# Row sums of mixing weights: added up by transfers in DRAM instead of products with ones

## Chip, cores and metric

The kernel runs on one core of a Trainium2 chip. The metric is the device time of one execution, in microseconds; the runs shown are three, and their median is the time before.

## What is computed

One layer of a streaming encoder: RMSNorm, one wide input projection, a sliding-window attention branch, a gMLP branch with spatial gating, gates, an output projection and a last RMSNorm. All in float32, with 1024 tokens and 1024 channels. The part that matters here is the spatial gating:

```python
def chunked_spatial_gating(u, v, w_s, b_s, ln_g, ln_b):
    v = layernorm(v, ln_g, ln_b)                      # (x - mu) * r * ln_g + ln_b
    vb = v.reshape(B, nb, SG_BLOCK, SG_GROUPS, SG_GROUP_WIDTH)
    mask = jnp.asarray(cidx[None, :] <= cidx[:, None])   # chunks of 64
    w = jnp.where(mask[None], w_s, jnp.zeros_like(w_s))
    mixed = jnp.einsum('gij,bnjgc->bnigc', w, vb) + jnp.transpose(b_s)[None, None, :, :, None]
    return u * mixed.reshape(B, S, SG_WIDTH)
```

Since `ln_b` is the same for every position j, its share of `mixed` is `ln_b[c]` times the sum of `w[g, i, j]` over j. So the kernel mixes only the normalized values and keeps, for each group g and row i, a bias: (row sum) x `ln_b` + `sg_b`. The row sums are 8 x 128 numbers, wanted in all 128 partitions (channels). The weights come as `sg_w[j, g, i]`; for j of 64 and above, only i of 64 and above counts.

## The kernel before

Every large product is a float32 product made of three products of split values (a rounded high part and a rest), and products of 2x2 blocks are done by a scheme of seven products on sums and differences (`b11`, `t1`, `t2`, `b21`, `t3`, `b22`, `t4`). A value is split by a cast on ACT (L176, `wh` or `T_..h`) and a subtraction on DVE (L177, `wl` or `T_..l`).

The stage that the change touches lies between 55 and 125 us. Until 94 us the projection of `vs`, the gMLP's gated input, is computed: L793 with weights `s1`, `s4`, then `late_product` (L1005) three times, for `t2`, `t3` and `t4`. Each call has two halves of the weights (c) and four token tiles (t), six matmuls each, and accumulates into four PSUM banks (`accs`: two of `ps_mm`, two of `ps_tp`). Between the calls' tiles other work is dealt out from a list (`aside`): splits of the next weights and forms, GELU on ACT, statistics on DVE. After the second half of each tile a step (`to_x12`, L1017, and `to_x22`, L1020) takes the bank's content away on DVE, and only then may the next call add to that bank. So in DVE's queue stand, one behind the other: the four `T_t2l`, the `wl` of the second half of t2, the `wl` of s3's first half, four `T_t3l`, then statistics and `to_x12` in turn.

From 94 us on `gemm_pair` (L371) does the projection of `u`, four pairs of seven products. Between its products `hook` (L1073) takes two entries at a time from a list `late`: second-half statistics of eight tiles, `normalize` (L1082), `bias_of` (L1089), and `mix` (L1105), which multiplies 128x128 blocks of normalized values by the mixing weights, adds the bias and stores the product with `u` to DRAM.

The row sums before: the mixing weights (tile `wT`, loaded at L969) get their masked corner set to zero (L1046), are split like any other weight (L1048), and four matmuls (L1059) multiply a 128x128 tile of ones (L1003) by the high and the low parts, 512 columns at a time. That leaves the row sums in all 128 partitions of two PSUM banks (`ps_sc`), which `bias_of` reads.

Transfers: SP issues plain loads and stores, in its own order. POOL issues the transfers that add (`accum_op`). Before 55 us these make sums of weights (L618: `T_t4h`, `T_t3h`, `T_t3l`) and sums of forms of the input (L618: `x` <- `T_t4l` at `add_on` in `second_tile`, `xh` <- `xh` in `raw_t2`). From 63 us on POOL adds up weights in DRAM for later phases (`early`, L316, one step at every second tile of `late_product`). An engine's queue runs in order: a POOL transfer that waits for another to land holds up all that POOL issues behind it. Eight semaphores are used in turn for the transfers of each kind of queue, so a transfer also waits for the one that had its semaphore before.

The order in which the instructions of an engine stand is not the order of the code: a scheduler places them by its own estimate of when their inputs are ready, and `after` (L99) adds constraints by hand.

Of the kernel before, what the change touches and what calls it, by code (L numbers as in the profile page):

```python
# [24 lines left out]
F32 = mybir.dt.float32  # L25
F32R = mybir.dt.float32r
AF = mybir.ActivationFunctionType
ALU = mybir.AluOpType
PSUM = bass.MemoryType.PSUM

P = 128
D = 1024
S = 1024
KC = D // P
HALF = 512
# [17 lines left out]
def hybrid_tile(  # L53
# [16 lines left out]
    nc = tc.nc  # L70
# [8 lines left out]
    def nm(s):  # L79
        count[0] += 1  # L80
        return f"{s}_{count[0]}"

    def bank(tag, dt=F32):
        return psum.tile([P, 512], dt, name=nm("ps_" + tag), tag="ps_" + tag, bufs=2)

    def mtile(shape, dt, tag, bufs, pool=None):
        return (pool or main).tile(shape, dt, name=nm(tag), tag=tag, bufs=bufs)

    def scratch(name, shape=(D, S)):
        return dram.tile(list(shape), F32, name=name)  # L90
# [4 lines left out]
    def xtile():  # L95
        return mtile([P, HALF], F32, "x", 5)


    def after(second, first):  # L99

        tc.add_manual_dep(
            second.ins,
            first.ins.name,
            mybir.DependencyInfo(mybir.DependencyClass.NoSync, mybir.DependencyReason.DATA),
            reason="order",
        )
# [6 lines left out]
    ident = const.tile([P, P], F32, name="ident")  # L113
# [21 lines left out]
    k_dr = scratch("k_dr", (P, 4, S))  # L135
    v_dr = scratch("v_dr", (NT, P, 2, 3 * HD))
    s1_dr = scratch("s1_dr")
    z_dr = scratch("z_dr")
    gs_dr = scratch("gs_dr")
    ga_dr = scratch("ga_dr")  # L140
# [28 lines left out]
    def split(hi, lo, src, minus=False):  # L169
        if minus:  # L170
            hi_of.append(nc.scalar.mul(hi, src, -1.0))
            return nc.vector.scalar_tensor_tensor(
                lo, src, -1.0, hi.bitcast(F32), op0=ALU.mult, op1=ALU.subtract
            )
        else:
            hi_of.append(nc.scalar.copy(hi, src))  # L176
            lo_of.append(nc.vector.tensor_sub(lo, src, hi.bitcast(F32)))  # L177
            return lo_of[-1]
# [32 lines left out]
    def copy_to(dst, src):  # L211
        nc.sync.dma_start(dst, src)
# [39 lines left out]
    def half_of(half):  # L252
        return slice(half * HALF, (half + 1) * HALF)
# [100 lines left out]
    def product(acc, part, form, fresh, last=True):  # L354
        wh, wl = part
        bh, bl = form
        for k in range(4):
            ks = slice(k * P, (k + 1) * P)
            for n, (lt, rt) in enumerate(
                ((wh[:, ks], bh[:, k, :]), (wh[:, ks], bl[:, k, :]), (wl[:, ks], bh[:, k, :]))  # L360
            ):
                nc.tensor.matmul(  # L362
                    acc,
                    lt,
                    rt,
                    start=fresh and k == 0 and n == 0,
                    stop=k == 3 and n == 2,
                    skip_group_check=True,
                )

    def gemm_pair(b, finish, hook=lambda: None, second="o"):  # L371

        n = done[0]
        done[0] += 1
        acc = bank("mm")[:]
        x11, x12, x22 = xtile(), xtile(), xtile()
        product(acc, ready[n, 0], b["b11"], True)
        pace[0] = nc.scalar.copy(x11[:], acc)  # L380
        hook()
        t5 = bank("o")[:]
        product(t5, ready[n, 2], b["t1"], True)
        pace[0] = nc.scalar.mul(x22[:], t5, -1.0)
        hook()
        product(acc, ready[n, 3], b["t2"], False)
        pace[0] = nc.scalar.copy(x12[:], acc)
        split_next()
        hook()
        t2 = bank(second)[:]  # L390
        product(t2, ready[n, 1], b["b21"], True)
        term[0] = term_of_x11[0] = nc.vector.tensor_add(x11[:], x11[:], t2)
        finish(0, 0, x11, x11[:], 1.0)
        split_next()
        hook()
        product(acc, ready[n, 4], b["t3"], False)
        term[0] = nc.vector.tensor_sub(x22[:], x22[:], acc)
        finish(1, 1, x22, x22[:], 1.0)
        hook()
        product(t5, ready[n, 5], b["b22"], False)  # L400
        term[0] = nc.vector.tensor_add(x12[:], x12[:], t5)
        finish(0, 1, x12, x12[:], 1.0)
        split_next()
        hook()
        product(acc, ready[n, 6], b["t4"], False)
        finish(1, 0, xtile(), acc, -1.0)
        split_next()
        hook()
# [102 lines left out]
    def part_of_early(every=2):  # L511
        hooks[0] += 1
        if early and hooks[0] % every == 0:
            early.pop(0)()
# [28 lines left out]
    pool = outer.enter_context(tc.tile_pool(name="mixing", bufs=1))  # L543
# [71 lines left out]
    casts, lows, turns, scalings, squares = [], [], [], [], []  # L615

    def add_on(dst, src):
        return nc.gpsimd.dma_start(dst, src, accum_op=ALU.add)  # L618
# [127 lines left out]
    def pair_of_w():  # L746
        return mtile([P, D], F32R, "wh", 3), mtile([P, D], F32R, "wl", 3)
# [5 lines left out]
    def split_w(name, c, src=None, behind=False):  # L753
        hi, lo = pair_of_w()
        (split_behind if behind else split)(hi[:], lo[:], flat(two_k(raws[name], c)) if src is None else src)
        keep_w(name, c, hi, lo)
# [211 lines left out]
    mix_w = mtile([P, KC, P], F32, "wT", 1, pool)  # L968
# [23 lines left out]
    def statistics(t, half):  # L992
        return nc.vector.bn_stats(stats[:, t, half, :], xh[:, t, half_of(half)])
# [5 lines left out]
            for i in range(2):  # L999
                after(statistics(t + i, 0), lows[-1])  # L1000

    ones = mtile([P, P], F32R, "ones", 1, pool)
    after(nc.vector.tensor_scalar(ones[:], ident[:], 0.0, 1.0, op0=ALU.mult, op1=ALU.add), lows[-1])  # L1003

    def late_product(name, weight, done, aside):  # L1005
        for c in range(2):
            for t in range(4):
                pace[0] = vs_product(accs[t], name, t, weight, False, cs=(c,))
                if t % 2:
                    part_of_early(1)  # L1010
                if c:
                    done(t)
                if aside:
                    aside.pop(0)()
# [16 lines left out]
    def part_of(name, t):  # L1031
        form_of(name, t, by_k(nf12[t][:] if name == "t3" else raw_b21(t)))
        if name == "t3" and t == 3:
            after(kept[3], casts[-1])

    late_product(
        "t2",
        "s2",
# [2 lines left out]
        + [lambda t=t: part_of("t3", t) for t in range(4)]  # L1041
        + [lambda: gelu_of(0), lambda: gelu_of(2)],
    )
    row_sums = [bank("sc") for half in range(2)]
    split_w("s3", 1)
    after(nc.vector.memset(mix_w[64:128, :, 0:64], 0.0), lows[-1])  # L1046
    wh, wl = pair_of_w()
    split(wh[:], wl[:], mix_w[:].rearrange("p g i -> p (g i)"))  # L1048
    late_product(
        "t3",  # L1050
        "s3",
# [2 lines left out]
        + [lambda t=t: part_of("t4", t) for t in range(4)]  # L1054
        + [lambda: split_w("a22", 0, a22[0][:]), lambda: gelu_of(4), lambda: gelu_of(6)],
    )
    for half in range(2):
        for n, part in enumerate((wh, wl)):
            nc.tensor.matmul(row_sums[half][:], ones[:], part[:, half_of(half)], start=n == 0, stop=n == 1)  # L1059
    split_w("a22", 1, a22[1][:])  # L1060
    part_of_early(1)
    begin_job()
# [8 lines left out]
    late = []  # L1071

    def hook():  # L1073
        for _ in range(2):
            if late:
                late.pop(0)()

    def statistics_of(t):
        statistics(t, 1)
        nc.vector.bn_aggr(mv[:, t, :], stats[:, t])  # L1080
# [8 lines left out]
    def bias_of(half):  # L1089

        wT = mix_w[:, half * 4 : half * 4 + 4, :]
        bg = first_bias
        if half:
            bg = mtile([P, 4, P], F32, "bias", 1, pool)
            nc.sync.dma_start(bg[:].rearrange("p g i -> p (g i)"), sg_b[half_of(half)].partition_broadcast(P))
        for gg in range(4):
            g = half * 4 + gg
            nc.vector.scalar_tensor_tensor(
                bg[:, gg, :], row_sums[half][:, gg * P : (gg + 1) * P], lb_sb[:, g : g + 1], bg[:, gg, :], op0=ALU.mult, op1=ALU.add
            )  # L1100
        return bg, wT
# [26 lines left out]
    def both():  # L1128
        part_of_early(1)
        hook()  # L1130

    late.extend(lambda t=t: statistics_of(t) for t in range(NT))
    late.append(normalize)
    for m in range(0, KC, 2):

        def finish(i, half, q, src, sign, m=m):
            nc.scalar.activation(q[:], src, AF.Gelu, scale=sign)
            late.append(lambda: mix(m + i, half, q))

        if m % 4 == 0:  # L1140
            late.append(lambda m=m: bias.append(bias_of(m // 4)))
        gemm_pair(hb, finish, both)
    while late:
        late.pop(0)()
# [5 lines left out]
    pool = stage.enter_context(tc.tile_pool(name="keys", bufs=1))  # L1150
# [44 lines left out]
    pool = stage.enter_context(tc.tile_pool(name="queries", bufs=1))  # L1195
# [210 lines left out]
    pool = stage.enter_context(tc.tile_pool(name="attention", bufs=1))  # L1406
# [234 lines left out]
    pool = stage.enter_context(tc.tile_pool(name="later", bufs=1))  # L1641
# [384 lines left out]
    for p in range(4):  # L2026
        n, t, acc, x11 = N_PAIRS + p, T_ORDER[p], accs[p], firsts[p]
# [93 lines left out]
        for e in range(2):  # L2121
            cs = slice(e * wide, (e + 1) * wide)
            part = bank("sc")[:, 0:wide]
# [95 lines left out]
```

## Time and profile before

| | |
|---|---|
| runs | 894.76, 895.32, 896.27 us (median 895.32) |
| profiled execution | 894.85 us, its span 893.0 us |
| granted TensorE clock | 0.999 |
| transfers | 212.40 MB, mean 238 GB/s |

How to read the lines that follow. Times are microseconds from the start of the span. PE is the engine of matmuls, DVE and ACT work on vectors, POOL and SP mostly issue transfers ("POOLq", "SPq" are their sequencers). A row of a timeline has start, duration, engine, line, operation, what is written <- read, the count, and in brackets how long the engine had been idle before and what ended that. Matmuls are pipelined: the row of one is longer than the distance to the next. A landing is the time from the issue of a transfer to its completion.

### The profile page before, as it was taken

Reading aid. Unit: us, or ns where it says so; the run is one execution under the profiler, and the core shown is the slowest. Engines: PE = TensorE matmul, PEld = TensorE weight load, DVE = VectorE, ACT = ScalarE, POOL = GpSimd, SP = SyncE. Lnnn points to the kernel's source line nnn. Section 1 sums busy time; section 2 is a strip of 40 time slices with the busy share of each in tenths; the row PEclk is TensorE's granted clock in tenths of the full one; section 3 lists DMA queues with packets and bytes.
Section 4 is the critical chain, followed back from the end, with each engine's and each line's share of the span. In section 5 each row is a group of like instructions: output and inputs, shape, how many; then the busy total and the mean of one; then the engine's idle time right before and its main releaser. Section 6 shows DMA issues by size and latency. Waiting matters only on the chain.

```text
span 893.0 us, 13163 instructions
## 1 busy us (share of the span) xinstructions
PE 883.5 (99%) x4117; PEld 731.3 (82%) x4117; DVE 684.9 (77%) x1362; ACT 581.0 (65%) x1189; POOL 151.4 (17%) x217
## 2 busy tenths in 40 slices
PE   9999999999999999999999999999999999999996
PEld 6888888888888888888888888888888888888885
DVE  7879966566686778888878888847796578579886
ACT  6875523334445489999889999955685385467443
POOL 3332222203030001111211011101121121110012
PEclk9999999999999999999999999999999999999999
DMA  9997888958778767888776789989899789998533
GB/s 329 221 276 211 269 204 172 175 153 266 246 253 289 213 186 190 209 190 195 176 229 215 239 223 236 237 286 378 317 292 375 271 232 257 298 309 282 178 119 118
DMA packets 131410, 212.40 MB, mean 238 GB/s; under 512 B 12778, under 2 KB 59882, under 8 KB 131340
## 3 DMA queue, kind: packets, MB, share of 16 engines
q1 hardware_dynamic: 108808, 148.62, 50.2%
q0 software_dynamic: 22384, 62.67, 31.6%
q8 instruction: 33, 0.54, 0.2%
q14 instruction: 37, 0.30, 0.1%
q10 hardware_dynamic: 148, 0.27, 0.1%
HBM read 146.37 MB, written 86.11 MB: 260 GB/s over the span
## 4 chain that ended last, share of the span: by engine, by line
PE 93%; ACT 3%; DVE 2%; issue 1%; DMA 1%; POOL 0%; SPq 0%; ACTq 0%
PE ps_mm L362 41%; PE ps_o L362 26%; PE ps_tp L362 7%; PE ps_sc L362 3%; PE ps_tp L793 2%; PE ps_o L793 2%; PE ps_mm L793 2%; PE ps_sc L1438 2%; PE ps_tp L1511 2%; PE ps_tp L1109 2%; PE ps_o L1546 2%; PE ps_sc L793 1%; PE ps_o L1551 1%; PE ps_sc L663 1%; ACT pr L1466 1%
## 5 line engine op out<-in xcount | busy, mean ns | idle before, releaser
L176 ACT CAST wh<-s 128x1024 fp32r<-128x1024 f32 (+1 forms) x79 | 79.4, 1006 | 77.4 <-PE ps_mm L362 27.7
L177 DVE TENSOR_TENSOR wl<-wr,wh 128x512 fp32r<-128x512 f32 (+1 forms) x77 | 72.0, 937 | 56.1 <-ACT wh L176 55.2
L177 DVE TENSOR_TENSOR wl<-s,wh 128x1024 fp32r<-128x1024 f32 (+1 forms) x79 | 92.5, 1170 | 9.6 <-ACT wh L176 9.6
L176 ACT CAST wh<-wr 128x512 fp32r<-128x512 f32 (+1 forms) x77 | 63.0, 819 | 55.3 <-PE ps_mm L362 30.7
L362 PE MATMUL ps_o<-T_t1h,wh 128*128 128x512 f32 x148 | 57.9, 391 | 0.0
L362 PE MATMUL ps_o<-T_t1h,wl 128*128 128x512 f32 x148 | 57.7, 390 | 0.0
L362 PE MATMUL ps_o<-T_t1l,wh 128*128 128x512 f32 x148 | 57.6, 389 | 0.0
L1444 ACT COPY sl<-ps_sc 128x384 f32<-128x384 f32 (+2 forms) x128 | 51.9, 456 | 7.0 <-DVE sm L1450 7.0
L1466 ACT ACTIVATE pr<-pr,sm 128x192 f32<-128x192 f32 (+2 forms) x128 | 56.2, 444 | 0.1
L1450 DVE CUSTOM_DVE_ANT_0 pr<-sl,nsink_sb 128x192 f32<-128x192 f32 (+2 forms) x128 | 48.0, 399 | 10.0 <-ACT sl L1444 8.9
L362 PE MATMUL ps_mm<-T_b11h,wh 128*128 128x512 f32 x140 | 55.0, 393 | 0.0
L362 PE MATMUL ps_mm<-T_t3h,wh 128*128 128x512 f32 x140 | 54.9, 392 | 0.0
L362 PE MATMUL ps_mm<-T_b11l,wh 128*128 128x512 f32 x140 | 54.6, 390 | 0.0
L362 PE MATMUL ps_mm<-T_t3h,wl 128*128 128x512 f32 x140 | 54.6, 390 | 0.0
L362 PE MATMUL ps_mm<-T_b11h,wl 128*128 128x512 f32 x140 | 54.6, 390 | 0.0
L362 PE MATMUL ps_mm<-T_t2l,wh 128*128 128x512 f32 x140 | 54.6, 390 | 0.0
L362 PE MATMUL ps_mm<-T_t2h,wh 128*128 128x512 f32 x140 | 54.6, 390 | 0.0
L362 PE MATMUL ps_mm<-T_t3l,wh 128*128 128x512 f32 x140 | 54.6, 390 | 0.0
L362 PE MATMUL ps_mm<-T_t2h,wl 128*128 128x512 f32 x140 | 54.5, 389 | 0.0
L362 PE MATMUL ps_mm<-T_t4h,wh 128*128 128x512 f32 x136 | 53.5, 393 | 0.0
L362 PE MATMUL ps_mm<-T_t4h,wl 128*128 128x512 f32 x136 | 53.1, 390 | 0.0
L362 PE MATMUL ps_mm<-T_t4l,wh 128*128 128x512 f32 x136 | 53.0, 389 | 0.0
(425 smaller groups left out, 2454.2 us busy)
## 6 DMA issues: line engine op xcount, KB each, us to landing
wr<-in_w_dram SPq DMA_DIRECT2D x86, 256.0 KB
sums<-in_w_dram POOLq DMA_DIRECT2D x20, 512.0 KB, 7.4
s<-sums SPq DMA_DIRECT2D x20, 512.0 KB
q_hl<-qhl SPq DMA_DIRECT2D x16, 512.0 KB
q<-q_hl SPq DMA_DIRECT2D x64, 128.0 KB
y_dr<-x POOLq DMA_DIRECT2D x28, 256.0 KB, 6.8
g<-in_w_dram POOLq DMA_DIRECT2D x12, 512.0 KB, 6.5
wr<-in_w_dram SPq DMA_DIRECT2D x11, 512.0 KB
```

Of the source, the lines that this page charges most:

```text
L176: hi_of.append(nc.scalar.copy(hi, src))
L177: lo_of.append(nc.vector.tensor_sub(lo, src, hi.bitcast(F32)))
L362: nc.tensor.matmul(acc, lt, rt, start=fresh and k == 0 and n == 0, stop=k == 3 and n == 2, skip_group_check=True,)
L663: turns.append(nc.tensor.transpose(pt[:, i * P : (i + 1) * P], xt[:, k * P : (k + 1) * P], ident[:]))
L793: mm = nc.tensor.matmul(acc[:], lt, rt, start=fresh and k == 0 and n == 0, stop=stops and k == 3 and n == terms[-1], skip_group_check=True,)
L1109: nc.tensor.matmul(pm[:, t * P : (t + 1) * P], xh[:, half * 4 + t, g * P : (g + 1) * P], bias[-1][1][:, g % 4, :], start=True, stop=True,)
L1438: nc.tensor.matmul(sc, q_of[:, c, i * P : (i + 1) * P], kt[:, :, lo:hi], start=True, stop=True)
L1444: copies.append(nc.scalar.copy(two, sc))
L1450: nc.vector.tensor_tensor_reduce(v, two[:, 0, :], two[:, 1, :], 1.0, nsk[:, i : i + 1], op0=ALU.add, op1=ALU.min, accum_out=nmax[:, c, i : ...
L1466: e = nc.scalar.activation(v, v, AF.Exp, bias=nmax[:, c, i : i + 1], scale=-1.0, accum_out=sums[:, c, i : i + 1])
L1511: nc.tensor.transpose(dst, pr[:, i, block * P : block * P + width], ident[:])
L1546: nc.tensor.matmul(po[:, first], va[1][:, vs], a[:, n, first], start=n == 0, stop=n == 1, skip_group_check=True)
```

## The change

The row sums are no longer products. In DRAM, a scratch `rs_dr` of 64 x 1024 gets the rows j = 0 to 63 by a plain copy (SP); the rows 64 to 127 are added to it by a transfer of POOL, only for i of 64 and above (which is the mask). Then six adding transfers of POOL halve the number of rows, 64 to 32, 16, 8, 4, 2 and 1; each needs the one before. At last two loads (SP) bring the 512 sums of each half from DRAM into a tile `rs` of 128 equal rows. The tile `ones`, the split of the mixing weights and the four matmuls are dropped. `bias_of` reads `rs` in place of PSUM. The tile `rs` has one buffer, so the second load waits until the first half's bias is made.

```diff
-    ones = mtile([P, P], F32R, "ones", 1, pool)
-    after(nc.vector.tensor_scalar(ones[:], ident[:], 0.0, 1.0, op0=ALU.mult, op1=ALU.add), lows[-1])
+    def add_rows(n):
+        return lambda: nc.gpsimd.dma_start(rs_dr[0:n], rs_dr[n : 2 * n], accum_op=ALU.add)
+
+    def first_rows():
+        copy_to(rs_dr[:], sg_w[0:64].rearrange("j g i -> j (g i)"))
+
+    def second_rows():
+        add_on(rs_dr[:].rearrange("j (g i) -> j g i", g=KC)[:, :, 64:P], sg_w[64:P, :, 64:P])
+
+    def load_row_sums(half):
+        row_sums.append(mtile([P, HALF], F32, "rs", 1, pool))
+        nc.sync.dma_start(row_sums[half][:], rs_dr[0][half_of(half)].partition_broadcast(P))
+
+    row_sums = []
+    first_rows()
+    adding = [None, second_rows]
+    for n in (32, 16, 8, 4, 2):
+        adding += [None, add_rows(n)]
...
                 if t % 2:
                     part_of_early(1)
+                elif adding:
+                    step = adding.pop(0)
+                    if step is not None:
+                        step()
...
-    row_sums = [bank("sc") for half in range(2)]
     split_w("s3", 1)
     after(nc.vector.memset(mix_w[64:128, :, 0:64], 0.0), lows[-1])
-    wh, wl = pair_of_w()
-    split(wh[:], wl[:], mix_w[:].rearrange("p g i -> p (g i)"))
...
-    for half in range(2):
-        for n, part in enumerate((wh, wl)):
-            nc.tensor.matmul(row_sums[half][:], ones[:], part[:, half_of(half)], start=n == 0, stop=n == 1)
...
+    assert not adding
+    late.append(add_rows(1))
     late.extend(lambda t=t: statistics_of(t) for t in range(NT))
+    late.insert(8, lambda: load_row_sums(0))
     late.append(normalize)
...
+        if m == 2:
+            late.append(lambda: load_row_sums(1))
```

What the scheduler makes of it, at two places. First POOL's queue before 63 us. `x` and `xh` are the sums of forms of the input, `T_t4h` the sum that becomes `s3`. Before:

```order
L618 DMA x_145<-T_t4l_400 128x512
L618 DMA xh_120<-xh_120 128x512
L618 DMA x_146<-T_t4l_400 128x512
L618 DMA xh_120<-xh_120 128x512
L618 DMA T_t4h_529<-in_w_dram 128x1024 x2
L618 DMA x_147<-T_t4l_400 128x512
L618 DMA xh_120<-xh_120 128x512
L618 DMA x_148<-T_t4l_400 128x512
L618 DMA xh_120<-xh_120 128x512
```

And in the changed kernel (there the numbers of tiles are higher by one; `rs_dr` is the scratch of the row sums, and the form tells how many rows are added):

```order
L619 DMA rs_dr<-in_sg_w_dram 512x64
L1004 DMA rs_dr<-rs_dr 16x2048
L1004 DMA rs_dr<-rs_dr 16x1024
L1004 DMA rs_dr<-rs_dr 16x512
L619 DMA x_146<-T_t4l_401 128x512
L619 DMA xh_121<-xh_121 128x512
L1004 DMA rs_dr<-rs_dr 16x256
L619 DMA x_147<-T_t4l_401 128x512
L1004 DMA rs_dr<-rs_dr 16x128
L619 DMA xh_121<-xh_121 128x512
L619 DMA T_t4h_530<-in_w_dram 128x1024 x2
L1004 DMA rs_dr<-rs_dr 16x64
```

So the seven adds stand much earlier than in the code: the first four ahead of all sums of forms, the last ahead of the third `x`.

Second, the load of the sums on SP and its reader on DVE. SP before, from the loads of the first weights of `u` on (`wr`):

```order
L212 DMA wr_909<-in_w_dram 128x512 x2
L212 DMA wr_910<-in_w_dram 128x512 x2
L212 DMA wr_991<-in_w_dram 128x512 x2
L212 DMA wr_992<-in_w_dram 128x512 x2
L212 DMA wr_1181<-in_w_dram 128x512 x2
```

SP in the changed kernel:

```order
L213 DMA wr_903<-in_w_dram 128x512 x2
L213 DMA wr_904<-in_w_dram 128x512 x2
L1014 DMA rs_1096<-rs_dr 128x512
L1014 DMA rs_1238<-rs_dr 128x512
L213 DMA wr_987<-in_w_dram 128x512 x2
L213 DMA wr_988<-in_w_dram 128x512 x2
```

DVE before, from the first `wl` of s2 on:

```order
L682 TENSOR_TENSOR wl_690<-T_t3h_163,wh_689 128x1024
L673 SCALAR_TENSOR_TENSOR T_t2l_694<-xh_120,T_t2h_693 128x4x128 x4
L1003 TENSOR_SCALAR ones_735<-ident 128x128
L177 TENSOR_TENSOR wl_728<-T_t3h_163,wh_727 128x1024
L177 TENSOR_TENSOR wl_744<-T_t4h_529,wh_743 128x1024
```

DVE in the changed kernel:

```order
L683 TENSOR_TENSOR wl_691<-T_t3h_164,wh_690 128x1024
L674 SCALAR_TENSOR_TENSOR T_t2l_695<-xh_121,T_t2h_694 128x4x128 x4
L1113 SCALAR_TENSOR_TENSOR bias_628<-rs_1096,lb_sb,bias_628 128x128 x4
L178 TENSOR_TENSOR wl_729<-T_t3h_164,wh_728 128x1024
L178 TENSOR_TENSOR wl_744<-T_t4h_530,wh_743 128x1024
```

The four bias operations of the first half now stand ahead of the second `wl` of s2; before, they stood among the statistics of the second halves (93 to 95 us). On PE the four products with ones are gone, and the first four mixings stand one product later: two behind the first pair's `t4` instead of ahead of it, two behind the second pair's `b11`.

More of the change, by code (lines that the diff above doesn't have):

```diff
@@ L137, in hybrid_tile @@
     s1_dr = scratch("s1_dr")
+    rs_dr = scratch("rs_dr", (64, D))
     z_dr = scratch("z_dr")
```

## Prediction

> **What bounds the kernel now.** I read the page first: the busy times, then the shares of the chain of waits.
>
> ```profile
> PE 883.5 (99%) x4117; PEld 731.3 (82%) x4117; DVE 684.9 (77%) x1362; ACT 581.0 (65%) x1189; POOL 151.4 (17%) x217
> PE 93%; ACT 3%; DVE 2%; issue 1%; DMA 1%; POOL 0%; SPq 0%; ACTq 0%
> ```
>
> PE works in 883.5 of 893.0 us and carries 93% of the chain. So whatever PE no longer does comes off the time, and whatever makes PE wait is added to it. Next come the stages around the change (the view by windows; its columns are PE, weight loads, DVE, ACT and POOL, each with its count, then clock, DMA share and GB/s).
>
> ```profile
> 60.00:66.00 6.00, 6.00 (x28) 4.97 (x27) 3.94 (x5) 6.00 (x10) 0.76 (x1) 1.00 1.07 333
> 66.00:72.00 6.00, 6.00 (x28) 4.96 (x27) 6.00 (x10) 2.77 (x3) 1.94 (x3) 1.00 0.85 255
> 72.00:83.00 11.00, 11.00 (x50) 9.10 (x49) 10.77 (x17) 7.13 (x9) 2.87 (x5) 1.00 0.67 186
> ```
>
> PE has no gap there at full clock, but from 66 us on DVE has none either (6.00 of 6.00, 10.77 of 11.00). A DVE that is held up before 66 us has nothing to catch up with except its lead over PE.
>
> **What is removed.** The timeline of PE gives the four products with ones, and two points that I need later.
>
> ```profile
> 66.02 0.62 PE L793 MATMUL ps_mm<-wl,T_t2h 128*128 128x512 f32 x2
> 75.08 0.61 PE L793 MATMUL ps_tp<-wh,T_t3h 128*128 128x512 f32 x2
> 81.89 0.39 PE L1059 MATMUL ps_sc<-wh,ones 128*128 128x512 f32 x1
> 82.82 0.62 PE L793 MATMUL ps_mm<-wh,T_t4h 128*128 128x512 f32 x2
> ```
>
> The rows say 0.39 us each, but they overlap: from the first of the four (81.89) to the product behind them (82.82) it is **0.93 us**, and that is all that PE saves. The split of the weights also goes: one cast on ACT, and one subtraction on DVE that the next fence shows at 75.35 (1.22 us). Neither engine is waited for at that place, so both count nothing by themselves; DVE's gives it back some lead after 75 us.
>
> **What is moved: the bias.** The order shows the four bias operations of the first half where `ones` was made, ahead of the `wl` that the second half of the t2 product reads. In the timeline of DVE:
>
> ```profile
> 58.45 0.22 DVE L1003 TENSOR_SCALAR ones<-ident 128x128 fp32r<-128x128 f32 x1
> 61.85 1.23 DVE L177 TENSOR_TENSOR wl<-T_t3h,wh 128x1024 fp32r<-128x1024 f32 x1 [3.19 <-ACT wh L176]
> 72.18 0.68 DVE L1017 TENSOR_TENSOR xh<-xh,ps_tp 128x512 f32<-128x512 f32 x1
> 75.35 1.22 DVE L177 TENSOR_TENSOR wl<-wT,wh 128x1024 fp32r<-128x1024 f32 x1
> 94.38 0.29 DVE L1098 SCALAR_TENSOR_TENSOR bias<-ps_sc,lb_sb,bias 128x128 f32<-128x128 f32 x1
> 94.59 0.68 DVE L993 BATCH_NORM_STATS2 bn<-xh 128x6 f32<-128x512 f32 x1
> ```
>
> A bias operation takes 0.29 us, with the next start 0.21 us behind it, so four take about 0.9 us, and they can't start before the load of the row sums has landed, at T. DVE's queue is in order, so T + 0.9 is when the `wl` starts that started at 61.85.
>
> What does that cost PE? Two leads are to be compared. This `wl` ends at 63.08 and PE first reads it at 66.02: a lead of 2.94 us. Behind it DVE runs without a gap up to the add that ends at 72.86, which empties the bank that PE's row at 75.08 writes: a lead of 2.22 us. (The other adds of that phase have more.) The smaller decides: PE's stall is T + 0.9 - 61.85 - 2.22, that is **T - 63.2 us**, nothing if T is earlier. Later DVE gets its 1.22 us back, so I look for no further loss.
>
> **When does T come?** The load stands behind a chain. On POOL: the add of the lower rows, and six adds, each waiting until the one before has landed. In POOL's timeline these follow the row at 34.77, so they start at about 35.6 us; in the order the transfers of the other rows stand between or behind them.
>
> ```profile
> 34.77 0.85 POOL L618 DMA_DIRECT2D T_t3l<-T_t3h  x1 [1.72 <-DVE T_b22l L677]
> 35.34 1.15 POOL L618 DMA_DIRECT2D x<-T_t4l  x1
> 45.31 0.86 POOL L618 DMA_DIRECT2D T_t4h<-in_w_dram  x1 [3.01 <-DMA T_t4h<-in_w_dram]
> 54.01 0.86 POOL L618 DMA_DIRECT2D xh<-xh  x1 [1.43 <-DVE xh L720]
> ```
>
> How long a link takes is read from the landings, asked for one issue at a time (the add at 35.34, the one at 45.31, the one at 54.01), and, for a small transfer on a quieter queue, from the copies of the keys (32 KB, 16 of them):
>
> ```profile
> x<-T_t4l POOLq DMA_DIRECT2D x1, 256.0 KB, 5.7
> T_t4h<-in_w_dram POOLq DMA_DIRECT2D x1, 512.0 KB, 9.7
> xh<-xh POOLq DMA_DIRECT2D x1, 256.0 KB, 10.2
> DMA to landing us min/median/max: 2.2/2.9/3.7
> ```
>
> None of these is a small add from DRAM to DRAM, so its price lies between 2.2 and 10.2 us. The first link goes behind the T_t3l adds as the 256 KB add did, and I give it that add's 5.7 us: 41.3. The next two find the queue nearly empty but the DMA engines busy; 4 us each, nearer to 2.9 than to 5.7: 49.3. Then the two x and xh adds, which before were issued from 35.34 on, go out, and the last three links stand in one queue with four such adds (1.05 MB) and the two T_t4h adds (1.05 MB). What that queue moves is in the DMA view, here 42 to 50, 52 to 60, 60 to 68 and 68 to 70 us (packets, MB, share; q0 is POOL's queue, q1 the hardware queue that SP issues to):
>
> ```profile
> q1 hardware_dynamic: 462, 1.71, 60.7%
> q0 software_dynamic: 312, 0.55, 41.2%
> q0 software_dynamic: 618, 1.56, 101.8%
> q1 hardware_dynamic: 620, 0.12, 14.1%
> q1 hardware_dynamic: 1104, 1.78, 61.2%
> q1 hardware_dynamic: 2, 0.00, 0.3%
> ```
>
> With the hardware queue on small packets POOL's queue moves 1.56 MB in 8 us, so 2.1 MB take 10.8 us and the last add lands near 49.3 + 10.8 + 2.2 = 62.3. With large packets beside it (1.71 MB in 462) POOL's queue makes only 0.55 MB in 8 us, and some 5 us more are added: 62 to 67 us.
>
> Then the load itself. SP has it behind the loads of the first weights of the next phase (SP's timeline, and a row of its waits):
>
> ```profile
> 48.50 0.35 SPq L969 DMA_DIRECT2D wT<-in_sg_w_dram  x1
> 59.84 0.33 SPq L212 DMA_DIRECT2D wr<-in_w_dram  x1
> 80.12 9.33 SPq L212 DMA_DIRECT2D wr<-in_w_dram  x4
> SPq L212 <- DMA sink_sb<-in_sinks_dram: 2.1, 1, 2.1
> ```
>
> Before, SP issued the fourth of these loads at 59.84, was done with that at 60.2, and waited 2.1 us for the sinks, whose semaphore the load now reuses: it can't be issued before 62.3. And the hardware queue goes in order: from 52 to 60 us it moved 0.12 MB of small rows, with the 512 KB of mixing weights (issued at 48.5) and the rest waiting behind; from 60 to 68 it moved 1.78 MB, about the size of the mixing weights, the bias and the four loads (0.52 + 0.26 + 1.05); after 68 nothing. The 256 KB of row sums queue behind these: at 1.78 MB in 8 us they end between 68.0 and 69.2. So both chains point to the same place: 62 to 67 plus 2.2 or more, and 68 to 69. I take **T = 69** (bounds 64.5, where nothing queues: 62.3 + 2.2; and 76, where each of seven links costs 5.7 us, that is 35.6 + 40 = 75.5, before the load).
>
> A rule against this reading of the chain: the Trainium skill, DMA: Bandwidth & Descriptors, section Anatomy of one DMA, gives a DMA from POOL about 2.0 us fixed plus its bytes over 436 GB/s. By it, as an estimate, seven links with 0.39 MB in all would take 15 us and end at 50.5 us, and the chain would not matter. The rows disagree for this stretch: by the rule 256 KB land after 2.6 us, here they took 5.7 and 10.2.
>
> **What else moves, at nothing.** The copy of the upper rows (256 KB, SP) goes out while SP waits for tile buffers, ahead of the last x tile; at 1.78 MB in 8 us it could cost that tile up to 1.2 us, but others stand ahead of it. The x and xh adds land some 5 us later; their readers on DVE stand behind the bias, so they are hidden as long as the bias is later. POOL's later sums slip too; their first reader is at 556.4:
>
> ```profile
> L212 SPq DMA_DIRECT2D s<-sums x20: 518/530/1077, 556.4 to 737.0; - x20
> 112.25 1.41 DVE L1117 SCALAR_TENSOR_TENSOR ps_tp<-ps_tp,lg_sb,bias 128x512 f32<-128x512 f32 x2
> 113.57 1.28 DVE L1125 TENSOR_TENSOR x<-x,ps_tp 128x512 f32<-128x512 f32 x2
> ```
>
> The list of late steps is two entries longer, so the first four mixings go one product later on PE: the same instructions, with others in between. DVE's two pairs of rows above (2.7 us) then come later, and the stores behind them free x buffers later, while the next writer is ACT, a product behind. If that cover were gone, it is a product's length, 2.7 us, at most. The second load waits for the first bias; SP's next load before was due at 80.12, long after.
>
> **The sum.** 894.85 us is the profiled execution's own time (span 893.0). Less 0.93, plus T - 63.2 = 5.8 at T = 69: **899.7 us**, 4.9 above. The median of the runs shown is 895.32, 0.47 above the profiled one and well inside their spread; I don't add it.
>
> **Rivals.**
> 1. *The chain is quick and the queues are empty* (the other side). Links of 2.9 us, as for the keys, end at 35.6 + 20.3 = 55.9. If then the load lands 2.2 us after 62.3, T is 64.5 and the stall 1.3: 895.2, no change. If SP's loads too are earlier and T is under 63.2, only the 0.93 is left: 893.9. It decides up to T = 65.9, where the loss passes 1.8 us. The landing rule above gives this case. For it: with the x adds held back, the hardware queue has the engines to itself from 42 us on. Against it: landings of 5.7 to 10.2 us in just this stretch, and 1.78 MB ahead of the load. Chance 0.19 for no change, 0.03 for a gain.
> 2. *Queueing, T from 66 to 72*, my forecast: 897 to 903. Chance 0.56.
> 3. *Both queues slow each other*: the T_t4h adds and the large loads overlap, T near 75: stall 11.8, 905.7. For it: 0.55 MB in 8 us beside large packets. Chance 0.22.
>
> That the row sums are not made by transfers is not a case: the order has no product with ones left.
>
> **How the numbers follow.** A measurement of this kernel can tell about 0.2%, 1.8 us, from no change. Faster by more than that is hardly possible, since PE saves 0.93: 0.03. Within it, T up to 65.9: 0.19. Slower: 0.78. The range goes from 894.0 (rival 1 without a stall) to 906.0 (rival 3, with T a little above 75).
>
> **What would show it.** In the new trace: no row with `ones`; the first bias row of DVE at 69, idle time of about 10 us before it put down to the load of `rs`; PE idle some 5 to 6 us in all between 66 and 76, at the `wl` of the second t2 half and at the bank that DVE empties last; the last add landing at 62 to 67. Wrong it would be if the bias starts before 63, or if PE has its gaps elsewhere, above all at the x adds or at the mixings after 110 us.

## The result and the profile after

The changed kernel takes **915.50 us** (median of 4 runs, 914.68 to 917.12) against 895.04 for the kernel before, run beside it (893.90 to 896.27): a ratio of **1.0232, 95% interval 1.0219 to 1.0244**. The forecast was 899.7 with a range of 894.0 to 906.0. Slower was right; the size, 20.5 us instead of 4.9, lies outside the range.

The page's busy times and chain of waits come first.

```profile
span 913.8 us, 13168 instructions
PE 886.0 (97%) x4113; PEld 732.3 (80%) x4113; DVE 684.4 (75%) x1360; ACT 580.3 (64%) x1188; POOL 157.5 (17%) x224
PE 86%; DMA 6%; ACT 3%; DVE 2%; POOL 1%; issue 1%; SPq 0%; ACTq 0%; POOLq 0%; DVEq 0%
```

PE's share of the chain fell from 93% to 86%, and 6% are now put down to transfers. PE's busy time rose by 2.5 us although it has four products fewer: something made it slower as well. The view by windows over the stretch of the prediction (same columns as there) shows both.

```profile
60.00:66.00 6.00, 6.00 (x28) 4.99 (x27) 0.00 (x0) 0.59 (x1) 4.10 (x7) 1.00 0.76 127
66.00:72.00 6.00, 1.45 (x4) 0.52 (x3) 0.00 (x0) 3.86 (x4) 6.00 (x8) 0.87 1.01 179
72.00:83.00 11.00, 0.22 (x1) 0.00 (x0) 0.00 (x0) 1.53 (x2) 0.20 (x1) 0.50 0.96 213
83.00:85.40 2.40, 0.00 (x0) 0.00 (x0) 2.27 (x6) 0.00 (x0) 0.00 (x0) 0.50 0.11 45
85.40:91.00 5.60, 5.54 (x13) 4.43 (x14) 5.60 (x10) 4.55 (x7) 0.60 (x1) 0.51 0.12 43
91.00:93.00 2.00, 2.00 (x10) 1.62 (x10) 1.99 (x4) 1.06 (x1) 0.09 (x1) 1.00 0.61 213
```

From 66 to 85.4 us PE has next to no work, and DVE does nothing at all from 60 to 83. When PE goes on, it does so at a granted clock of 0.50 until about 91. PE's timeline gives the two waits and the first products of t3 and t4:

```profile
71.00 1.22 PE L794 MATMUL ps_mm<-wh,T_t2h 128*128 128x512 f32 x2 [4.55 <-ACT wh L177]
85.46 1.22 PE L794 MATMUL ps_mm<-wl,T_t2h 128*128 128x512 f32 x2 [13.25 <-DVE wl L178]
93.12 0.62 PE L794 MATMUL ps_mm<-wh,T_t3h 128*128 128x512 f32 x2
104.00 0.62 PE L794 MATMUL ps_mm<-wh,T_t4h 128*128 128x512 f32 x2
```

The first product that reads the second `wl` of t2 came at 66.02 and now comes at 85.46: **+19.44**. From there to the first product of t3 it was 4.98 us (66.02 to 71.00) and is 7.66 (to 93.12): **+2.68**, the half clock. From t3 to t4 it was 11.82 and is 10.88: **-0.94**, the four products with ones. That makes 21.18; the span grew by 20.8, so 0.4 comes back later. What DVE waits for stands in its timeline:

```profile
83.13 1.14 DVE L1113 SCALAR_TENSOR_TENSOR bias<-rs,lb_sb,bias 128x128 f32<-128x128 f32 x4 [23.89 <-DMA rs<-rs_dr]
84.19 1.22 DVE L178 TENSOR_TENSOR wl<-T_t3h,wh 128x1024 fp32r<-128x1024 f32 x1
```

T, the landing of the row sums, is 83.1 and not 69. POOL's timeline has the chain (five of its seven links: the lower rows, then the adds of 32, 16, 8 and, last, one row):

```profile
35.92 1.38 POOL L619 DMA_DIRECT2D rs_dr<-in_sg_w_dram  x1
42.97 0.79 POOL L1004 DMA_DIRECT2D rs_dr<-rs_dr  x1 [5.66 <-DMA rs_dr<-in_sg_w_dram]
48.63 0.77 POOL L1004 DMA_DIRECT2D rs_dr<-rs_dr  x1 [4.88 <-DMA rs_dr<-rs_dr]
56.62 0.76 POOL L1004 DMA_DIRECT2D rs_dr<-rs_dr  x1 [7.22 <-DMA rs_dr<-rs_dr]
65.61 1.53 POOL L1004 DMA_DIRECT2D rs_dr<-rs_dr  x1
```

Taken one issue at a time, the first three of these took 6.8, 5.4 and 7.7 us to land, the next three 2.3 to 3.3, and the last 7.5. The view of the adds' line has the six of them:

```profile
DMA to landing us min/median/max: 2.3/4.3/7.7
```

SP issued the load at 73.27, as soon as the last add had landed; it took 9.8 us. (The group has both loads of row sums; the second was issued at 84.30.)

```profile
73.27 11.35 SPq L1014 DMA_DIRECT2D rs<-rs_dr  x2
```

And ACT, which the prediction did not look at, waits too: its copies of `xh` stand behind the adds that POOL held back, and its casts of weights stand behind these copies.

```profile
67.07 0.58 ACT L845 COPY xh<-ps_o 128x512 f32<-128x512 f32 x1 [4.05 <-DMA xh<-xh]
69.92 1.03 ACT L177 CAST wh<-T_t3h 128x1024 fp32r<-128x1024 f32 x1
75.65 0.58 ACT L845 COPY xh<-ps_sc 128x512 f32<-128x512 f32 x1 [4.70 <-DMA xh<-xh]
```

### The profile page after: what moved, and what is told of

Its sections match the earlier page's. It is cut to its first block, busy times and chain, and to the rows that moved or that the text cites. A ratio compares the mean times of both kernels' runs of the same rounds, so it can differ in the third digit from the quotient of the medians.

```text
span 913.8 us, 13168 instructions
## 1 busy us (share of the span) xinstructions
PE 886.0 (97%) x4113; PEld 732.3 (80%) x4113; DVE 684.4 (75%) x1360; ACT 580.3 (64%) x1188; POOL 157.5 (17%) x224
## 4 chain that ended last, share of the span: by engine, by line
PE 86%; DMA 6%; ACT 3%; DVE 2%; POOL 1%; issue 1%; SPq 0%; ACTq 0%; POOLq 0%; DVEq 0%
PE ps_mm L363 40%; PE ps_o L363 25%; PE ps_tp L363 7%; PE ps_sc L363 3%; DMA T_t4h<-in_w_dram 2%; PE ps_sc L1458 2%; PE ps_tp L1531 2%; DMA rs_dr<-rs_dr 2%; PE ps_mm L794 2%; PE ps_tp L1124 2%; PE ps_tp L794 2%; PE ps_o L1566 2%; DMA sums<-in_w_dram 1%; DMA rs_dr<-in_sg_w_dram 1%; POOL xh L619 1%
```

## The experiments

Two explanations stood against each other at first. **A**: the bias stands too early in DVE's in-order queue, and waits there for a load that comes at the end of a long chain. **B**: the chain stands too early in POOL's queue and holds back the x and xh adds, so that ACT comes late; where the bias stands does not matter. The times below are medians, each with its ratio to the kernel before, which ran beside it at 894.62 to 894.71.

### The bias put back behind the statistics

```
+        aggregates.append(nc.vector.bn_aggr(mv[:, t, :], stats[:, t]))
...
+            if half == 0:
+                after(made, aggregates[-1])
```

> The four bias operations of the first half of the channels are put back behind the last of the statistics on DVE, where they stood before the change; the chain of adds on POOL, the loads and everything else stay as in the changed kernel. Theory A (the cost is the place of the bias in DVE's queue, ahead of the wl of the second t2 half, with a load that lands at 83.1 us): the 13.25 us wait of PE at that wl goes. What is left is the wait for the copies of xh on ACT that stand behind the late xh adds (4.55 us before the second t2 half, in the changed kernel at 71.0), a few us more at t3 for the same reason, and some time at half clock behind these gaps: 901 to 903 us. Rival B (the chain's place in POOL's queue is the cost, because it holds back the x and xh adds, and the bias's place does not matter): within 2 us of the changed kernel, 914 to 917.

Measured: **907.86 us**, 1.0145 (1.0131 to 1.0158). DVE no longer waits for the load, and PE's long wait is gone; two shorter ones are left (PE's timeline, then windows behind the second of them):

```profile
71.49 1.22 PE L794 MATMUL ps_mm<-wh,T_t2h 128*128 128x512 f32 x2 [4.77 <-ACT wh L177]
82.91 0.71 PE L794 MATMUL ps_mm<-wh,T_t3h 128*128 128x512 f32 x2 [3.08 <-DVE xh L1038]
```

```profile
84.00:85.00 1.00, 1.00 (x4) 0.81 (x3) 1.00 (x2) 1.00 (x2) 0.00 (x0) 0.50 0.76 256
85.00:86.00 1.00, 1.00 (x4) 0.71 (x4) 1.00 (x3) 0.98 (x2) 0.00 (x0) 0.50 0.54 221
```

Neither theory holds alone: 7.6 of the 20.5 us went, 13.2 are left without any wait for the bias. They are the two waits (7.85) and two spells at half clock (about 5.1 and 3.4 us long, half of which is lost, 4.3); t2 began at 61.12 instead of 60.12, and the saving of 0.9 goes off again. That makes 12.2 of the 12.9 us by which the span grew; 0.7 stay unexplained. So the two costs lie side by side in the changed kernel: while PE waited for the bias, most of the wait for the xh adds was hidden behind it.

### No row sums, the bias late: the floor

The edit takes out the copy, the adds and the loads, and pins the bias as above.

> As the kernel without row sums (they are left out, a constant tile stands in their place), and the four bias operations of the first half stand behind the statistics on DVE. Nothing is added to any queue and the four products with ones are gone: the most that the change could gain. Both theories: 0.93 us less than before the change, 893.9 to 894.4.

Measured: **893.91 us**, 0.9989 (0.9980 to 0.9998). PE's saving is real and is all there is to gain: 0.8 us, where 0.93 was expected.

### No row sums, the bias early

The same, without the pin. There the scheduler put the bias one step further ahead, before the T_t2l subtractions.

> The row sums are left out: no copy, no adds and no loads of them, a constant tile stands in their place (so the bias comes out from ones). The bias operations keep their early place on DVE and now wait only for the load of the bias weights, which stands behind the mixing weights in the hardware queue. Theory A says that the stall is the landing less 63.2 us: with a landing near 66.5 us (the hardware queue was drained at about 68 before the change) some 2 to 4 us of PE wait, plus up to 1 us at half clock, less 0.93: 896 to 898. If the landing is before 63.2, or rival B holds: the pure saving, 893.9 to 894.4.

Measured: **902.87 us**, 1.0094 (1.0075 to 1.0113), above what was expected. PE waited 6.06 us for T_t2l (at 67.45) and lost 1.6 at half clock. Even without any chain the place is too early: the load of the bias weights itself landed at 65.7. To test the formula the bias had to stand exactly where the changed kernel has it:

```
+    last_t2l = lows[-1]
...
+            if half == 0:
+                after(made, last_t2l)
```

> The row sums are left out (no copy, adds or loads of them, a constant tile in their place, so the bias comes out from ones), and the bias operations stand exactly where the changed kernel has them, behind the four T_t2l subtractions. They wait only for the load of the bias weights, which landed at 65.66 in the kernel without row sums whose bias stood one step earlier. By the forecast's formula the stall is 65.7 - 63.2 = 2.5 us; if waits of PE under about 3 us leave the clock full, that is all: 894.7 - 0.9 + 2.5 = 896.3; with a spell at half clock 898 to 899. If the place does not matter: 893.9.

Measured: **896.18 us**, 1.0019 (1.0007 to 1.0031). The timelines of DVE and PE:

```profile
64.86 1.14 DVE L1112 SCALAR_TENSOR_TENSOR bias<-rs,lb_sb,bias 128x128 f32<-128x128 f32 x4 [6.56 <-DMA bias<-in_sg_b_dram]
67.19 0.73 PE L794 MATMUL ps_mm<-wl,T_t2h 128*128 128x512 f32 x2 [1.24 <-DVE wl L178]
76.72 0.70 PE L794 MATMUL ps_tp<-wh,T_t3h 128*128 128x512 f32 x2
```

And the window in which that wait lies:

```profile
64.00:68.00 4.00, 2.76 (x13) 1.96 (x12) 3.14 (x6) 0.83 (x2) 0.72 (x1) 1.00 1.10 394
```

With T = 64.9 the formula gives 1.7 us. PE waited 1.24 at the `wl`, and the product behind the bank that DVE empties last, at 75.08 before, came at 76.72, 1.64 us later. The clock stayed at 1.00.

### The chain behind the x and xh adds

```
+        last_form_sum = raw_t2(t)
...
+        move = add_on(rs_dr[:].rearrange("j (g i) -> j g i", g=KC)[:, :, 64:P], sg_w[64:P, :, 64:P])
+        after(move, last_form_sum)
```

> The chain of adds on POOL starts only behind the last of the adds that form the sums in x and xh; with that the scheduler also puts the bias on DVE behind the statistics and the load of the row sums on SP behind eight loads of weights. Theory A and rival B both expect the changed kernel's loss to go: A because DVE meets no wait ahead of its t2 and t3 work, B because the x and xh adds go out as early as before the change. What is left is the saving of the four products, 0.93 us, if the load lands before the bias is wanted near 93 us, or before the first mixing wants it near 110: 893.9 to 894.6. If the load is later than that (a chain of seven links of 2.3 to 7.7 us from about 55 us, then 9.8 us of load, so 81 to 119), up to 9 us of wait appear at the first mixings: up to 904.

Measured: **907.82 us**, 1.0142 (1.0128 to 1.0156), worse than the worst case expected. No wait is left before 104 us, where PE stops until 111.72: the chain, which starts at 54.81 now, lands later than the bias is wanted (the timelines of POOL, SP, DVE and PE):

```profile
69.63 0.79 POOL L1004 DMA_DIRECT2D rs_dr<-rs_dr  x1 [13.43 <-DMA rs_dr<-in_sg_w_dram]
89.66 3.60 POOL L317 DMA_DIRECT2D sums<-in_w_dram  x5
97.69 0.33 SPq L1015 DMA_DIRECT2D rs<-rs_dr  x1
107.13 0.35 DVE L1114 SCALAR_TENSOR_TENSOR bias<-rs,lb_sb,bias 128x128 f32<-128x128 f32 x1 [13.83 <-DMA rs<-rs_dr]
111.72 0.80 PE L363 MATMUL ps_mm<-T_t3h,wh 128*128 128x512 f32 x1 [7.65 <-ACT x L388]
```

The first link landed only at 69.6, behind the adds queued ahead of it; the last, beside five sums, at 97.5; the load took 9.4 us beside more sums. The statistics wait behind the bias, the normalization behind them; and ACT takes a root of these statistics (it waits 12.06 us for them) ahead of the copy that empties PE's bank. PE lost 7.65 and 1.52 us in waits and 2.2 at half clock: the 11.3 by which this span (903.9) is above the floor's (892.6).

### POOL's sums behind the chain

The chain stays where the last kernel has it; the calls that issue sums during t2 to t4 are taken out, and the sums go out in twos among the mixings.

> As the kernel whose chain starts behind the last of the adds that form the sums in x and xh, but POOL's later sums (the transfers of line 317) stand behind the whole chain, and go out in twos among the mixings. In the kernel before this one the links took 2.2 to 8.4 us each with sums queued between them, the last add landed at 97.5 and the load, beside sums, at 107.1. If the queue that the links share with the sums is what makes them slow, the six later links now cost 2.3 to 3.3 us each: second add landing near 69.6 as there, last add near 69.6 + 6 x 3.6 = 91 at most and 86 at best, load of 3 to 4 us, so 89 to 95, about when DVE wants it (93) and well before the first mixing (110): 893.9 to 895. If a link costs what it does whatever else is queued: last add near 97, load 100 to 107, some 0 to 8 us of wait: 894 to 907 with the links of 5 us and more seen in the trace.

Measured: **917.48 us**, 1.0258 (1.0244 to 1.0272), above both ranges expected. The chain did what was expected: the landings (view of the adds' line), then the load and the bias, without a wait, in the timelines, then two windows:

```profile
DMA to landing us min/median/max: 2.1/2.6/3.2
```

```profile
86.91 0.33 SPq L1015 DMA_DIRECT2D rs<-rs_dr  x1
91.46 0.30 DVE L1107 SCALAR_TENSOR_TENSOR bias<-rs,lb_sb,bias 128x128 f32<-128x128 f32 x1
```

```profile
60.00:110.00 50.00, 50.00 (x223) 41.39 (x222) 46.25 (x80) 29.80 (x40) 12.71 (x18) 1.00 0.57 147
160.00:220.00 60.00, 46.37 (x208) 38.13 (x207) 27.66 (x41) 15.11 (x22) 18.12 (x23) 0.89 0.93 192
```

PE has no gap from 60 to 110 us. The time was lost behind it: from 160 to 220 PE worked 46.4 of 60 us. The suspect is the crowd of sums among the mixings, which the experiment itself brought in. So the next kernel sends the sums out one at a time as before, and the thirteen left over during the attention phase (`part_of_early(1)` for `part_of_early()` there).

> As the kernel with POOL's sums behind the chain (917.5), whose chain was quick (links of 2.1 to 3.2 us, bias at 91.5 without a wait) but whose sums then went out two at a time among the mixings, with some 20 us of PE waits behind them. Here they go out one at a time as in the changed kernel, and the thirteen that are left over go out between 350 and 480 us. If the 20 us came from the crowd of sums among the mixings and not from the chain or the row sums: back to the floor, 893.9 to 895, as long as the attention phase takes the sums without waits; a few us more if not. If the row sums made by transfers have another cost of that size that was hidden so far: above 905.

Measured: **894.14 us** (893.24 to 898.50), 0.9993 (0.9984 to 1.0002): the floor again, with the row sums made by transfers. The chain landed like the last one (2.1 to 3.4 us for each of the six later links), the bias started at 92.31 without a wait. The 23 us of the kernel before this one were the crowded sums. Against the kernel before the change this version can't be told from no change. Its trace is of a longer execution (897.90 us): there PE waited 1.67 and 1.78 us for loads of `q` in the attention phase (at 480.63 and 497.96), which no other trace here has. Whether the moved sums cause that is not shown.

### The wait on DVE alone

As the kernel with sums in twos, but the `wl` of the second t2 half is pinned behind the bias, so that the bias stands where the changed kernel has it, while the x and xh adds go out in time.

```
+    behind_bias = lo_of[-1]
...
+                after(behind_bias, made)
```

> As the kernel with POOL's sums behind the chain, whose x and xh adds go out ahead of the chain, but the four bias operations are kept where the changed kernel has them on DVE, ahead of the wl of the second t2 half. So only the wait on DVE is left of the change's two costs. Theory A: the stall is T - 63.2 with T the landing of the load; chain from 54.8, second add landed near 69.6, six links of about 2.8 us, load of 3 to 4: T near 90, stall near 27, 2.7 us more at half clock, less 0.93: 916 to 928, and whatever T is, the span is 892.1 + (T - 63.2) + 2 to 3. Rival B (the place of the bias does not matter once the x and xh adds are on time): 894 to 896.

Measured: **944.74 us**, 1.0566 (1.0549 to 1.0583), above the 916 to 928 of theory A; the crowd of sums, which this expectation did not count, is in this time too, so the partner is the 917.48 of the kernel that differs by the pin alone: **27.3 us**. The same three timelines:

```profile
84.92 4.55 SPq L1016 DMA_DIRECT2D rs<-rs_dr  x2
87.99 1.14 DVE L1108 SCALAR_TENSOR_TENSOR bias<-rs,lb_sb,bias 128x128 f32<-128x128 f32 x4 [29.86 <-DMA rs<-rs_dr]
90.31 1.22 PE L794 MATMUL ps_mm<-wl,T_t2h 128*128 128x512 f32 x2 [23.18 <-DVE wl L178]
```

T is 88.0, so the formula gives 24.8; with 5.3 us at half clock (90.3 to 95.6), half of it lost, 27.4. Rival B, by which the pin changes nothing (894 to 896, or 917.5 with the crowd), is out as the only cause.

### The chain between the adds, and in two parts

First the chain starts behind the fourth x and xh add, and its links stand among the others (`after(move, last_of_h)` at the lower rows).

> The chain of adds starts behind the fourth of the x and xh adds (in the changed kernel: ahead of all of them), and its links stand between the T_t4h adds, the last four x and xh adds and the first sums; the scheduler then puts the bias behind the statistics again. Nothing that ACT waits for stands behind more than two links. Theory A with its two causes (the bias's place, and the adds held back on POOL): most of the loss goes; a link waits for the T_t4h adds ahead of it (about 10 us each as landed before), so the chain ends at 75 to 90 and the load lands before 93: 894 to 897, the upper end if one of the last xh adds comes late for ACT's copy. If it is not the held adds, but the links themselves that slow everything: above 900.

Measured: **899.41 us**, 1.0059 (1.0046 to 1.0071), above the range expected, for the reason named there: one xh add still stood behind links (issued at 69.39), and ACT's GELU behind its copy.

```profile
69.39 1.18 POOL L619 DMA_DIRECT2D xh<-xh  x1
73.00 0.59 ACT L845 COPY xh<-ps_sc 128x512 f32<-128x512 f32 x1 [1.39 <-DMA xh<-xh]
74.53 1.19 PE L794 MATMUL ps_mm<-wh,T_t3h 128*128 128x512 f32 x2 [3.64 <-ACT xh L998]
```

Then the lower rows alone go there, and the six other links stand behind the last xh add, with sums between them.

> The chain in two parts: the add of the lower rows goes out behind the fourth of the x and xh adds, where POOL's queue is nearly empty (it landed before 54.5 there), and the six other links start only behind the last xh add, with the first sums between them; the bias stands behind the statistics. With the chain between the adds, PE still waited 3.64 us at t3 for a late xh add; here no add that ACT or DVE reads waits for a link. Theory A in its present form (two costs: the bias's place, and the x and xh adds held back; a chain kept off both is free as long as the load lands before about 110): links of 3 to 6 us from 54.5, the first behind four 256 KB adds, last add at 80 to 90, load of 4 to 10 us: no PE wait, the floor of 893.9 to 894.5. If the load is later than 110 or if the transfers themselves slow something: 895 to 900.

Measured: **895.81 us** (893.54 to 901.60), 1.0020 (1.0005 to 1.0035): near the floor but not on it. The load, issued at 85.13 beside seven sums, took 11.3 us; the bias waited for it, and PE waited 1.90 us at the first pair's `t4` product, for the bank that DVE empties (L398) behind the late statistics and normalization.

```profile
85.13 0.33 SPq L1015 DMA_DIRECT2D rs<-rs_dr  x1
96.46 0.35 DVE L1112 SCALAR_TENSOR_TENSOR bias<-rs,lb_sb,bias 128x128 f32<-128x128 f32 x1 [4.97 <-DMA rs<-rs_dr]
110.55 0.50 PE L363 MATMUL ps_mm<-T_t4h,wh 128*128 128x512 f32 x1 [1.90 <-DVE x L398]
```

## Why the prediction was wrong

- **PE's saving, 0.93 us**: right. 0.94 in the trace after, 0.8 by the floor.
- **The formula, a stall of T - 63.2**: right, each of its two leads where it counted. Where the clock stayed full (T = 64.9) PE waited first at the `wl` and then at the bank that DVE empties last; behind that bank it was 1.64 us late in all, by the formula 1.7. At T = 83.1 and 88.0 PE went on at half clock, and no wait is left at that bank; only the lead of the `wl`, 2.94 us, counted. That makes T - 63.9, so 19.2 and 24.1; the `wl` product came 19.4 and 24.3 us later than before the change. Two small misreadings cancel: from the first bias to the `wl` it is 1.06 us and not 0.9, and DVE was not without a gap behind the `wl` (0.21 us at 63.28).
- **T = 69: the step that failed**, by 14.1 us, 6.5 of them from the chain and 7.6 from the load behind it. The *chain*: the last add was to land at 62 to 67 and landed at 73.1; the first three links took 6.8, 5.4 and 7.7 us, not 5.7, 4 and 4, and the last one, behind the T_t4h adds, 7.5. The *load's place in the hardware queue*: it was costed behind 1.78 MB, but SP's loads had gone out earlier (the four weight loads at 49.2 to 53.2, not up to 59.8), and that queue was empty. The *load itself*: "plus 2.2 or more" was 9.8, with POOL's queue full beside it. The upper bound of 76 counted seven links of 5.7 us, which is close to what they took (37.2 us in all, 5.3 each), but no load behind them; so the range stopped short.
- **The clock**: the prediction counted waits only. PE's spell at 0.50 cost 2.7 us more.
- **"The x and xh adds land some 5 us later; hidden"**: half right. As long as the bias is later they cost little, as said; but the reader was sought on DVE alone, and ACT's copies at line 845, with the casts of weights behind them, were missed. PE's gap of 4.55 us ahead of 71.00 is theirs, and gaps at the x adds were one of the prediction's own signs of being wrong. Once the bias is out of the way these adds cost 12 us (two waits and two spells at half clock).
- **Rival 1**, a quick chain with 2.9 us a link, is not impossible as such: with POOL's sums out of the way and SP's queue nearly quiet the six later links took 2.1 to 3.4 us. At this place it did not hold. The estimate from the Trainium skill (DMA: Bandwidth & Descriptors, Anatomy of one DMA), 2.0 us and the bytes, comes near those links (2.0 to 2.3 us by it) and to none of the first three here.
- **Costed at nothing and so found**: the copy of the upper rows, the second load and the later mixings; the kernel with all three and the chain off both critical paths is at 894.14. T2 began 0.7 us later than before (60.84); kernels without the early chain vary from 59.67 to 60.52 there. PE lost 0.80 us at 46.46, after ACT had waited 1.30 us for the T_t3l add; the kernel with the bias put back, whose chain is as early, has a gap of 0.73 us there, and no other has one. That points to the early chain; no run tests it.
- **Rivals and forecast**: the likeliest case was queueing up to T = 72, the next T near 75. The case that came true, a slow chain and then a slow load one after the other, was bounded away.

## What to carry to other kernels

An instruction with a new input takes its old neighbours hostage: in an in-order queue, what counts is when its input lands against the slack of the instructions behind it, and both must be read on every engine that holds such a queue (here DVE for the bias, POOL for the chain, ACT for the copies behind POOL's adds). A chain of dependent transfers is to be costed link by link beside what the queues carry then, with its last load counted again at the end; the same seven links took 31 to 43 us here. And where a change removes 0.9 us from a busy engine, a wait of 3 us on it costs the wait and half of the next few microseconds.

## What the runs showed of the hardware

**The clock after a wait.** All the traces together have 14 waits of PE from 2.89 to 23.18 us (the shortest are 2.89, 3.03, 3.08, 3.39 and 3.64). After each of them PE ran at a granted clock of 0.50; where it could run on undisturbed that lasted 3.2 to 5.9 us. After most of the short ones the clock fell only when PE had started again, up to 1.2 us later; after waits of 4.55 us and more it was down already. After waits of 1.24, 1.52, 1.90, 2.27 and 2.77 us it stayed at 1.00. The Trainium skill (TensorE: Matmul & The Clock Gate, Part 1: The HAM clock gate) puts the fall to half rate at an idle window of about 3.4 us and the way back at as much; here a wait of 2.89 us was already enough, and the spell was up to 5.9 us.

**One load, three prices.** The same 256 KB of repeated row took 9.8 us in the changed kernel and 3.07 us with nothing beside it (84.92 to 87.99 above). The DMA view shows what was beside it, first the changed kernel from 74 to 83 us, then the kernel with the wait on DVE alone from 85 to 88:

```profile
q0 software_dynamic: 665, 1.69, 78.5%
q1 hardware_dynamic: 144, 0.26, 13.9%
```

```profile
q1 hardware_dynamic: 144, 0.26, 29.3%
```

It is the same 144 packets; with 2.08 MB from POOL's queue beside it the load took 11.3 us. That a full queue of POOL's makes SP's load three times as long is thus shown by pairs of runs, not by an experiment of its own. For the small adds it is argued the same way: 5.4 and 7.7 us while the hardware queue had 69.5% of the engines (43 to 56 us, after), 2.1 to 3.2 where it had 12.4% (75 to 87, sums behind the chain). No run changed SP's loads alone.
